# Strassen's scheme for layer B's V projection, woven with K's chunks, and K and V kept in DRAM

## The chip, the cores and the metric

The kernel runs on one core of one Trainium2 chip. The metric is the device time of one execution in microseconds (us). Engines are called as the profile calls them: PE is TensorE (PEld its weight loads), DVE VectorE, ACT ScalarE, POOL GpSimd, SP SyncE, which here only issues transfers.

## The reference, cut to what matters

A decoder trunk of two layers on 256 tokens of width 2048, all in 32-bit floats. Layer A is retention and attention to a memory of 256 tokens. Then one projection makes three keys and three values, which layer B's dilated attention reads:

```python
def shared_kv(x, g, w_kv):
    parts = split_cols(rmsnorm(x, g) @ w_kv, [DIL_W] * (2 * len(DIL_CONFIG)))

def dilated_layer(x, g, w_in, w_mem_kv, w_out, mem_n, kv):
    h = rmsnorm(x, g)
    parts = split_cols(h @ w_in, [DIL_W] * n_g + [DIL_W, MEM_W, MEM_W])
...
    for gi, (window, dil) in enumerate(DIL_CONFIG):
        q = parts[gi].reshape(B, S, DIL_HEADS, DIL_DH)
        o, lse = dilated_group(q, kv[2 * gi], kv[2 * gi + 1], dil, window // dil)
...
    return x + jnp.concatenate([o_dil, o_mem], axis=-1) @ w_out
```

K and V are each 256 x 2048 by 2048 x 6144. The norm is a row factor and a weight per column of x; both layer B's own norm and the one of K and V read the same x, with other weights.

## The kernel before, in words

**Numbers in two parts.** Every operand of a large product is split into a high part (ACT's cast to fp32r, line 94) and a low part (DVE's subtraction, line 95), and three products of parts are summed in PSUM: high by high, high by low, low by high.

**Chunks.** A projection is cut into chunks of 512 output columns. For one chunk eight weight tiles of 128 x 1024 come by SP's queue into a ring of six buffers (`raw`, RAW = 6), and each is split into `wh` and `wl`, rings of three (`wspl`). The splits are given AHEAD = 100 places of priority, so the scheduler puts them earlier in ACT's and DVE's streams than the work written before them.
- `dense_cols` (q, K, gates) gives features by tokens. It works in two halves of 256 features, with four weight tiles each; per tile eight pairs of a matmul of 512 columns (line 299) and one of 256 (line 301). A half ends with `fold`: ACT copies one part out of PSUM (344), DVE adds the other (345); K is then scaled by the tokens' norm (375). Two PSUM buffers, `acc0` and `acc1`, take turns.
- `dense` (V, gates of layer A, out-projections) gives tokens by features: per weight tile 12 matmuls of 512 columns (lines 316 to 318), then the scaled copies out of PSUM (385, 392, 393).

**Norm weights.** In layer B they are applied to the weights: `split_weights` runs in pieces of 256 or 512 columns with a factor per partition (lines 242, 243), once for GB and once for GK.

**Order.** For each of four head groups: q, K, q, K, q, K (seven chunks with the gate behind them), three V chunks, the gate. The attention of a group is a generator whose pieces `step()` sets between the next group's matmuls. `big` is a pool of 34 tiles of 512 KB in which x, the split x, K, V and what attention needs live.

Of the kernel before, what the change touches and what calls it, by code (L numbers as in the profile page):

```python
# [27 lines left out]
def yoco_trunk_kernel(  # L28
    ctx: ExitStack,
    tc: tile.TileContext,  # L30
    x, xt, memt,
    w_ac, w_ar, w_oa, w_b, w_ob, w_mk, w_mv, w_kc, w_vr,
    g_a, g_b, g_mem, g_kv, g_f,
# [11 lines left out]
    psum = ctx.enter_context(tc.tile_pool(name="psum", bufs=1, space=bass.MemoryType.PSUM))  # L45
    turns = {"acc": 0, "att": 0}

# [33 lines left out]
    def acc_tile(name=None):  # L81
        if name is None:
            name = ("acc0", "acc1")[turns["acc"] % 2]
            turns["acc"] += 1
        return psum.tile([P, 2, 2, S], F32, name=name)

    def bank():
        turns["att"] += 1
        if turns["att"] % 3 == 0:
            return acc_tile("acc2")[:, 0].rearrange("p h s -> p (h s)")  # L90
        return psum.tile([P, 512], F32, name="att", bufs=2)
# [20 lines left out]
    def drain():  # L112
        while pending:
            step()

    gain = const.tile([P, 4, KT], F32, name="gain")
# [173 lines left out]
    def dense_cols(xs, w, c, evict, g=None):  # L290
        for i in range(2):
            ps = acc_tile()
            for j in range(4):
                part = xs[j]
                for a, (wh, wl) in enumerate(weights(w[c, i, j], g, 4 * j, 4)):
                    first, last = j == 0 and a == 0, j == 3 and a == 3
                    for ct in range(2):
                        cs = slice(ct * P, (ct + 1) * P)
                        pe.matmul(ps[:, ct].rearrange("p h s -> p (h s)"), lhsT=wh[:, cs], rhs=xhl(part, a),  # L299
                                  start=first, stop=False, skip_group_check=True)  # L300
                        pe.matmul(ps[:, ct, 0, :], lhsT=wl[:, cs], rhs=xh(part, a),  # L301
                                  start=False, stop=last, skip_group_check=True)
# [60 lines left out]
    def cols_scaled(b, *job):  # L363
        o = big_tile()

        def evict(i, ps):
            fold(half(o, i), ps)
            if b is not None:
                scale_half(o, i, b)

# [244 lines left out]

    def turn_cols(xr, part):
        for i in range(2):
            ps = bank()
            for ct in range(2):
                for t in range(2):  # L620
                    cs = slice((2 * i + ct) * P, (2 * i + ct + 1) * P)
                    pe.transpose(ps[:, ct * S + t * P:ct * S + (t + 1) * P], xr[:, t, cs], ident)
            split(part[i][:, :, 0, :], part[i][:, :, 1, :], two(ps))
            yield

    n_m, n_x = Norm("m"), Norm("x")
# [66 lines left out]

    x1, ys = [], []
    part = const.tile([P, 2, 4], F32, name="part")
    ORDER = (4, 5, 0, 1, 2, 3)
    for c in range(4):
# [7 lines left out]
        x1.append(xr)  # L705
        ys.append(cols_pair())
        pending.append(turn_cols(xr, ys[c]))

    n_y = Norm("y")

    def norm_y():
# [6 lines left out]
        yield  # L718

    pending.append(norm_y())  # L720
    mkb2, mvb2 = {}, {}

    def split_big_rows(o):
        h, l = big_pair()
        h, l = rows(h), rows(l)
        f = "p t c -> p (t c)"
        split(h.rearrange(f), l.rearrange(f), o.rearrange(f))
        return h, l

    def split_kv(c):  # L730
        mkb2[c] = split_big(mk_b[c])
        yield
        h, l = split_big_rows(mv_b[c])
        mvb2[c] = (h, l)
        yield

    mix = SplitMix()
    for c in range(2):
        pending.append(split_kv(c))
        mq = cols_plain2(ys, w_b, 16 + c, GB)  # L740
        drain()
        gm = gate_cols(n_y.bh, ys, w_b, 18 + c, GB)
        pending.append(mem_attention(mq, mkb2[c], mvb2[c], gm, n_y, mix.tile(4 + c)))
    for hg in range(4):
        q, k, v = [], [], []
        for i in range(3):
            q.append((cols_plain2 if i == 0 else cols_plain)(ys, w_b, 4 * i + hg, GB))
# [7 lines left out]
        gt = gate_cols(n_y.bh, ys, w_b, 12 + hg, GB)  # L755
        pending.append(dilated(q, k, v, gt, n_y.nsd, mix.tile(hg)))

    part2 = const.tile([P, 2, 4], F32, name="part")

# [50 lines left out]
def _tables(np):  # L810
# [22 lines left out]

_ORDER = ["x", "xt", "memt", "w_ac", "w_ar", "w_oa", "w_b", "w_ob", "w_mk", "w_mv", "w_kc", "w_vr",
          "g_a", "g_b", "g_mem", "g_kv", "g_f", "rope", "decay", "mask"]
# [59 lines left out]
```

## Time and profile before

| | us |
|---|---|
| median of 3 runs (lowest, highest) | 1917.36 (1916.36, 1919.44) |
| the profiled execution's own time | 1918.47 |
| its span, first to last instruction | 1916.7 |
| busy in it: PE / PEld | 1900.3 / 1630.2 |
| DVE / ACT / POOL | 1240.2 / 1093.6 / 13.2 |
| mean granted clock of PE | 0.997 of full speed |

How to read it: busy time is the union of an engine's instructions. Matmuls overlap in the records (one of 512 columns has a mean of 390 ns, though they start closer together), so the pace of PE is read from how many start in a stretch. A mean over the whole span hides stages with other limits; so stretches are read by themselves.

### The profile page before, as it was taken

To read this page: it belongs to the slowest core of one execution; us is meant where nothing else is said; L and a number is where in the kernel's file an instruction comes from. 1 tells how busy PE (TensorE), PEld (TensorE's weight loads), DVE (VectorE), ACT (ScalarE), POOL (GpSimd) and SP (SyncE) were. 2 spreads that over 40 slices of the span, in tenths; PEclk is the share of its full clock that TensorE was granted. 3 is DMA by queue.
4 is the path that set the end of the run, shared out by engine and by line. 5 is a ranking of instruction groups with operands and counts; after the bars stand their busy time and mean duration, and the time that the engine had idled before them with its cause. 6 is when DMAs were issued, how large, how long until landed. Compare 5 with 4: busy or idle time off the path is not lost.

```text
span 1916.7 us, 27329 instructions
## 1 busy us (share of the span) xinstructions
PE 1900.3 (99%) x10136; PEld 1630.2 (85%) x10136; DVE 1240.2 (65%) x2191; ACT 1093.6 (57%) x2035; POOL 13.2 (1%) x24
## 2 busy tenths in 40 slices
PE   9999999999999999999999999999999999999998
PEld 7888888888888888888888988889888898888886
DVE  6566567557555457776656776567765777657654
ACT  6455444455444447766656666566665666656543
POOL 1000000000000000000000000000000000000000
PEclk9999999999999999999999999999999999999999
DMA  8565654655666665545665466654566546565463
GB/s 278 190 231 187 187 161 158 205 180 167 207 186 195 201 187 177 164 154 188 187 196 178 132 191 194 188 186 132 189 189 195 177 141 193 188 193 181 143 202 122
DMA packets 102805, 349.68 MB, mean 182 GB/s; under 512 B 11296, under 2 KB 17488, under 8 KB 102672
## 3 DMA queue, kind: packets, MB, share of 16 engines
q1 hardware_dynamic: 102208, 347.12, 57.4%
q8 instruction: 79, 1.29, 0.3%
q0 software_dynamic: 320, 0.81, 0.1%
q14 instruction: 54, 0.44, 0.1%
q10 hardware_dynamic: 144, 0.01, 0.0%
HBM read 345.80 MB, written 2.10 MB: 182 GB/s over the span
## 4 chain that ended last, share of the span: by engine, by line
PE 97%; DMA 1%; issue 1%; ACT 1%; DVE 1%; SPq 0%; POOL 0%; ACTq 0%; POOLq 0%; DVEq 0%
PE acc L299 33%; PE acc L301 17%; PE acc L318 13%; PE acc L317 13%; PE acc L316 13%; DMA raw<-in_w_mk_dram 1%; PE att L98 1%; PE att L100 1%; PE att L99 1%; PE att L599 1%; PE att L585 0%; PE att L563 0%; PE acc L100 0%; PE acc L99 0%; PE acc L98 0%
## 5 line engine op out<-in xcount | busy, mean ns | idle before, releaser
L299 PE MATMUL acc<-big,wh 128*128 128x512 f32 x2752 | 976.4, 399 | 2.0 <-DVE big L345 2.0
L301 PE MATMUL acc<-big,wl 128*128 128x256 f32 x2752 | 770.2, 280 | 0.0
L243 DVE SCALAR_TENSOR_TENSOR wl<-raw,gain,wh 128x256 fp32r<-128x256 f32 (+1 forms) x1216 | 567.4, 524 | 307.5 <-ACT wh L242 307.1
L242 ACT ACTIVATE wh<-raw,gain 128x256 fp32r<-128x256 f32 (+1 forms) x1216 | 567.2, 533 | 343.4 <-PE acc L299 176.9
L299 PEld LDWEIGHTS acc<-big,wh 128*128 128x128 f32 x2752 | 517.6, 188 | 122.5 <-DVE big L345 2.1
L95 DVE TENSOR_TENSOR wl<-raw,wh 128x1024 fp32r<-128x1024 f32 (+1 forms) x290 | 346.4, 1195 | 295.9 <-ACT wh L94 295.4
L301 PEld LDWEIGHTS acc<-big,wl 128*128 128x128 f32 x2752 | 519.7, 189 | 0.3
L94 ACT CAST wh<-raw 128x1024 fp32r<-128x1024 f32 (+1 forms) x290 | 298.1, 1028 | 380.0 <-PE acc L318 229.8
L316 PE MATMUL acc<-wh,big 128*128 128x512 f32 x1128 | 441.5, 391 | 0.0
L317 PE MATMUL acc<-wl,big 128*128 128x512 f32 x1128 | 439.6, 390 | 0.0
L318 PE MATMUL acc<-wh,big 128*128 128x512 f32 x1128 | 439.4, 390 | 0.0
L318 PEld LDWEIGHTS acc<-wh,big 128*128 128x128 f32 x1128 | 211.8, 188 | 44.0
L316 PEld LDWEIGHTS acc<-wh,big 128*128 128x128 f32 x1128 | 211.9, 188 | 43.2
L317 PEld LDWEIGHTS acc<-wl,big 128*128 128x128 f32 x1128 | 211.9, 188 | 42.6
L345 DVE TENSOR_TENSOR big<-acc,big 128x512 f32<-128x512 f32 x64 | 44.0, 689 | 0.0
L344 ACT COPY big<-acc 128x512 f32<-128x512 f32 x64 | 36.3, 568 | 0.7 <-PE acc L284 0.6
L95 DVE TENSOR_TENSOR big<-big 128x512 fp32r<-128x512 f32 (+1 forms) x34 | 28.0, 843 | 2.9 <-ACT big L94 2.8
L571 ACT ACTIVATE p<-sm,mn 128x512 f32<-128x512 f32 x32 | 23.1, 722 | 5.7 <-DVE mn L567 5.7
L94 ACT CAST big<-big 128x512 fp32r<-128x512 f32 (+1 forms) x34 | 24.3, 744 | 2.2 <-DVE big L601 2.0
L282 PE MATMUL acc<-big,wh 128*128 128x512 f32 x64 | 22.8, 400 | 1.3 <-ACT wh L94 1.3
L375 DVE TENSOR_TENSOR big<-big,nb 128x512 f32<-128x512 f32 x32 | 21.9, 691 | 1.0
L98 PE MATMUL att<-big 128*128 128x256 f32 x77 | 22.0, 286 | 0.0
(204 smaller groups left out, 930.9 us busy)
## 6 DMA issues: line engine op xcount, KB each, us to landing
raw<-in_w_b_dram SPq DMA_DIRECT2D x160, 512.0 KB, 3.5
raw<-in_w_kc_dram SPq DMA_DIRECT2D x96, 512.0 KB, 3.5
raw<-in_w_vr_dram SPq DMA_DIRECT2D x96, 512.0 KB, 3.5
raw<-in_w_ac_dram SPq DMA_DIRECT2D x64, 512.0 KB, 3.5
raw<-in_w_ar_dram SPq DMA_DIRECT2D x64, 512.0 KB, 3.5
raw<-in_w_oa_dram SPq DMA_DIRECT2D x48, 512.0 KB, 3.5
raw<-in_w_ob_dram SPq DMA_DIRECT2D x48, 512.0 KB, 4.1
raw<-in_w_mv_dram SPq DMA_DIRECT2D x32, 512.0 KB, 3.5
```

Source lines behind the costliest of these rows:

```text
L94: act.copy(hi, src)
L95: dve.tensor_tensor(lo, src, hi.bitcast(F32), ALU.subtract)
L98: pe.matmul(o, lhsT=ah, rhs=bh, start=first, stop=False, skip_group_check=True)
L242: act.activation(wh[:, cs], raw[:, cs], AF.Copy, scale=gs)
L243: dve.scalar_tensor_tensor(wl[:, cs], raw[:, cs], gs, wh[:, cs].bitcast(F32), ALU.mult, ALU.subtract)
L299: pe.matmul(ps[:, ct].rearrange("p h s -> p (h s)"), lhsT=wh[:, cs], rhs=xhl(part, a), start=first, stop=False, skip_group_check=True)
L301: pe.matmul(ps[:, ct, 0, :], lhsT=wl[:, cs], rhs=xh(part, a), start=False, stop=last, skip_group_check=True)
L316: pe.matmul(ps[t], lhsT=xh(part, a)[:, ts], rhs=wh, start=first, stop=False)
L317: pe.matmul(ps[t], lhsT=xh(part, a)[:, ts], rhs=wl, start=False, stop=False)
L318: pe.matmul(ps[t], lhsT=xl(part, a)[:, ts], rhs=wh, start=False, stop=last)
L344: act.copy(two(out), ps[:, :, 1, :])
L345: dve.tensor_tensor(two(out), ps[:, :, 0, :], two(out), ALU.add)
```

## The change

- V is computed by Strassen's scheme (in Winograd's form) on pairs of chunks: tokens in two halves of 128, the inner dimension in two of 1024, the columns in two of 512. Seven products of half size take the place of eight. The combinations of x (`combine`) are made once; those of the weights (`s1`, `w12 + w22`, `s2`, `s2 + w21`) by DVE for each pair, a quarter `d` at a time: three additions and four products for each of four `d` (first part), then one addition and three products for each of four (second part). PSUM banks `acc1` and `acc2` hold the sums; `p12` and `p` tiles the first combinations of results.
- All 12 K chunks come first, one after the other. From the second on, `weave` sets products between them: 2, 2, 1 and 0 behind a half's four weight tiles and 3 behind its fold. So a half has 8 products, and the 6 x 28 products fit into 21 of 22 halves. While products are left, K uses `acc0` alone, and `bank()` two buffers in place of three.
- K, V, x and the memory's K and V for layer B are stored to DRAM on POOL's queue (`spill`) and fetched by it (`fetch`) where they are used.
- Norm weights are applied to y (`Scaled`), for K and V and again for layer B; the weights are split whole, without a factor.

```diff
-            name = ("acc0", "acc1")[turns["acc"] % 2]
+            name = ("acc0", "acc1")[0 if woven else turns["acc"] % 2]
...
+                weave((2, 2, 1, 0)[j])
             evict(i, ps)
+            weave(3)
+
+    def strassen(parts, comb, w, r, done, banks=[]):
...
+        def product(ps, src, x, d, start, stop):
+            wh = wspl.tile([P, 1024], F32R, name="wh")
+            wl = wspl.tile([P, 1024], F32R, name="wl")
+            ahead(split, wh, wl, src)
+            for i in range(2):
+                h, l = x(2 * d + i)
+                cs = slice(i * 512, (i + 1) * 512)
+                first, last = start and i == 0, stop and i == 1
+                pe.matmul(ps, lhsT=h, rhs=wh[:, cs], start=first, stop=False, skip_group_check=True)
+                pe.matmul(ps, lhsT=h, rhs=wl[:, cs], start=False, stop=False, skip_group_check=True)
+                pe.matmul(ps, lhsT=l, rhs=wh[:, cs], start=False, stop=last, skip_group_check=True)
...
+        for d in range(4):
+            w11, w12, w22 = (load(q, d) for q in range(3))
+            s1, s2 = flat(big_tile()), flat(big_tile())
+            ahead(dve.tensor_tensor, s1, w11, w12, ALU.add)
+            ahead(dve.tensor_tensor, w12, w12, w22, ALU.add)
+            ahead(dve.tensor_tensor, s2, s1, w22, ALU.add)
+            keep.append(s2)
+            f, l = d == 0, d == 3
+            product(b0, w12, com(7), d, f, l)
...
+            product(b1, s1, com(5), d, f, l)
...
+            product(b2, w22, com(3), d, f, l)
+            yield
+            product(b3, w11, own(0, 0), d, f, l)
+            if l:
+                dve.tensor_tensor(c5, c5, b3, ALU.subtract)
+                dve.tensor_tensor(o1[:, 1, :], b3, c7, ALU.subtract)
+                dve.tensor_tensor(o2[:, 0, :], b2, c5, ALU.add)
+                dve.tensor_tensor(o2[:, 1, :], c7, c5, ALU.add)
+            yield
+        for d in range(4):
+            w21, s2 = load(3, d), keep[d]
+            product(b0, s2, com(6), d, f, l)
...
+            ahead(dve.tensor_tensor, s2, s2, w21, ALU.add)
+            product(b1, s2, own(1, 1), d, f, l)
...
+            product(b3, w21, own(1, 0), d, False, l)
...
+    def spill(t):
+        d = dram.tile([P, 1024], F32, name=f"spill{turns['spill']}")
+        pool.dma_start(out=d, in_=t)
...
+    for i in range(3):
+        for hg in range(4):
+            kd[i, hg] = spill(flat(cols_scaled(lambda: n_y.b, yk, w_kc, 4 * i + hg)))
+            if first:
+                drain()
+                first = False
+                for p in range(6):
+                    woven.append(strassen(yk, comb, w_vs[p], n_y.r, done(p)))
...
+    for j in range(4):
+        pending.append(yb.start(j))
...
-            kk = cols_scaled(n_y.b, ys, w_kc, 4 * i + hg, GK)
+            kk = fetch(kd[i, hg])
             k.append(split_big(kk) if i == 0 else kk)
-        for i in range(3):
-            v.append((rows_scaled2 if i == 0 else rows_scaled)(dense(ys, w_vr, 4 * i + hg, GK), n_y.r))
+            vv = fetch(vd[i, hg])
+            v.append(split_big_rows(vv) if i == 0 else rows(vv))
```

What it moves is seen in the built program's order. In the changed kernel's rows L97 is the subtraction of a split (95 before), L352 the additions of weight tiles, L457 fold's addition (345 before), L487 K's scaling (375 before), L310 and L312 a column chunk's matmuls (299 and 301 before), and L362 to L364 a product's.

First place, DVE where a K half ends. Before, four weight tiles are split between two folds (head group 0, K's first chunk and its second half):

```order
L243 SCALAR_TENSOR_TENSOR wl_8118<-raw_8115,gain_76,wh_8117 128x256 x4
L243 SCALAR_TENSOR_TENSOR wl_8151<-raw_8148,gain_76,wh_8150 128x256 x4
L243 SCALAR_TENSOR_TENSOR wl_8179<-raw_8176,gain_76,wh_8178 128x256 x4
L243 SCALAR_TENSOR_TENSOR wl_8207<-raw_8204,gain_76,wh_8206 128x256 x4
L345 TENSOR_TENSOR big_7913<-acc1_8030,big_7913 128x512
L375 TENSOR_TENSOR big_7913<-big_7913,nb_6094 128x512
```

Now, in the third K half among the first products: the first row is the split of that half's last weight tile (`raw_6468`), the fold stands near the end:

```order
L97 TENSOR_TENSOR wl_6471<-raw_6468,wh_6470 128x1024
L97 TENSOR_TENSOR wl_6494<-big_6453,wh_6493 128x1024
L97 TENSOR_TENSOR wl_6504<-raw_6451,wh_6503 128x1024
L352 TENSOR_TENSOR big_6552<-raw_6546,raw_6548 128x1024
L97 TENSOR_TENSOR wl_6514<-raw_6447,wh_6513 128x1024
L97 TENSOR_TENSOR wl_6527<-raw_6524,wh_6526 128x1024
L352 TENSOR_TENSOR big_6553<-big_6552,raw_6550 128x1024
L352 TENSOR_TENSOR raw_6548<-raw_6548,raw_6550 128x1024
L457 TENSOR_TENSOR big_6324<-acc0_6325,big_6324 128x512
L487 TENSOR_TENSOR big_6324<-big_6324,nb_6153 128x512
```

Between them now stand three products' splits (`wl_6494`, `wl_6504`, `wl_6514`), three additions, and the split of the next half's first tile (`wl_6527`).

Second place, PE at such an end. Before, the next half starts in the other PSUM buffer:

```order
L299 MATMUL acc0_7914<-big_6008,wh_8001 128x512
L301 MATMUL acc0_7914<-big_6008,wl_8002 128x256
L299 MATMUL acc0_7914<-big_6008,wh_8001 128x512
L301 MATMUL acc0_7914<-big_6008,wl_8002 128x256
L299 MATMUL acc1_8030<-big_5284,wh_8033 128x512
L301 MATMUL acc1_8030<-big_5284,wl_8034 128x256
```

Now three products stand between two K halves (the last of them here), and the next half writes `acc0` again, which the fold above has to leave first:

```order
L362 MATMUL acc2_6349<-wh_6513,big_5332 128x512
L363 MATMUL acc2_6349<-wl_6514,big_5332 128x512
L364 MATMUL acc2_6349<-wh_6513,big_5332 128x512
L362 MATMUL acc2_6349<-wh_6513,big_5332 128x512
L363 MATMUL acc2_6349<-wl_6514,big_5332 128x512
L364 MATMUL acc2_6349<-wh_6513,big_5332 128x512
L310 MATMUL acc0_6523<-big_5331,wh_6526 128x512
L312 MATMUL acc0_6523<-big_5331,wl_6527 128x256
```

So PE cannot begin a K half, as it did, while the former half is being read out.

Third place, DVE in the second part of a pair: the addition of `w21` stands one row ahead of the split of its sum, whose high part ACT casts in between:

```order
L97 TENSOR_TENSOR wl_7574<-big_7237,wh_7573 128x1024
L352 TENSOR_TENSOR big_7237<-big_7237,raw_7571 128x1024
L97 TENSOR_TENSOR wl_7585<-big_7237,wh_7584 128x1024
L97 TENSOR_TENSOR wl_7597<-raw_7594,wh_7596 128x1024
L97 TENSOR_TENSOR wl_7617<-raw_7571,wh_7616 128x1024
L97 TENSOR_TENSOR wl_7629<-raw_7626,wh_7628 128x1024
L97 TENSOR_TENSOR wl_7654<-big_7336,wh_7653 128x1024
L352 TENSOR_TENSOR big_7336<-big_7336,raw_7651 128x1024
L97 TENSOR_TENSOR wl_7670<-big_7336,wh_7669 128x1024
```

Before, no split waited for an addition; each followed a cast of a loaded tile.

## Rows read from the trace of the kernel before

**Rows 1.** Page: span, and each engine's busy time, share of the span, instructions.
```profile
span 1916.7 us, 27329 instructions
PE 1900.3 (99%) x10136; PEld 1630.2 (85%) x10136; DVE 1240.2 (65%) x2191; ACT 1093.6 (57%) x2035; POOL 13.2 (1%) x24
```

**Rows 2.** Windows, microseconds: out-projection A; a head group's K and q; its V; the next's K.
```profile
core 0: us, PE busy (x) PEld busy (x) DVE busy (x) ACT busy (x) POOL busy (x), PEclk, DMA share, GB/s
...
480.00:715.00 235.00, 233.79 (x1088) 194.60 (x1087) 128.53 (x142) 108.53 (x143) 2.73 (x4) 1.00 0.62 195
...
957.50:1022.70 65.20, 65.20 (x290) 54.01 (x289) 37.09 (x56) 35.66 (x57) 0.00 (x0) 1.00 0.61 193
1022.80:1195.40 172.60, 172.60 (x1041) 152.44 (x1041) 124.01 (x289) 116.01 (x272) 0.00 (x0) 1.00 0.55 171
1195.40:1260.70 65.30, 65.30 (x290) 54.09 (x289) 37.08 (x56) 35.64 (x57) 0.00 (x0) 1.00 0.60 193
```

**Rows 3.** Page part 4: the chain that ended last, by engine and by line.
```profile
PE 97%; DMA 1%; issue 1%; ACT 1%; DVE 1%; SPq 0%; POOL 0%; ACTq 0%; POOLq 0%; DVEq 0%
PE acc L299 33%; PE acc L301 17%; PE acc L318 13%; PE acc L317 13%; PE acc L316 13%; DMA raw<-in_w_mk_dram 1%; PE att L98 1%; PE att L100 1%; PE att L99 1%; PE att L599 1%; PE att L585 0%; PE att L563 0%; PE acc L100 0%; PE acc L99 0%; PE acc L98 0%
```

**Rows 4.** Windows of line 316 alone: one of three V matmuls, in two V stretches.
```profile
957.50:1022.70 65.20, 37.35 (x96) 17.96 (x96) 1.00 0.61 193
1195.40:1260.70 65.30, 37.36 (x96) 17.98 (x96) 1.00 0.60 193
```

**Rows 5.** Windows of line 299 alone: two column chunks of 64 wide matmuls each.
```profile
100.75:146.00 45.25, 45.20 (x128) 23.88 (x128) 1.00 0.69 233
```

**Rows 6.** DVE by line and shape: busy us, mean ns of one | idle before.
```profile
L243 DVE SCALAR_TENSOR_TENSOR wl<-raw,gain,wh 128x256 fp32r<-128x256 f32 x1024 | 431.7, 482 | 192.4 <-ACT wh L242 192.4
L95 DVE TENSOR_TENSOR wl<-raw,wh 128x1024 fp32r<-128x1024 f32 x274 | 335.4, 1224 | 293.1 <-ACT wh L94 292.7
...
L345 DVE TENSOR_TENSOR big<-acc,big 128x512 f32<-128x512 f32 x64 | 44.0, 689 | 0.0
...
L574 DVE TENSOR_SCALAR p<-p,rl 128x512 f32<-128x512 f32 x32 | 15.4, 483 | 0.6
...
L459 DVE TENSOR_SCALAR p<-p,rl 128x256 f32<-128x256 f32 x16 | 4.9, 348 | 0.1
...
L768 DVE TENSOR_TENSOR big<-big,p 128x512 f32<-128x512 f32 x8 | 5.2, 682 | 0.0
```

**Rows 7.** DVE in order of time: two operations of 1024 columns, back to back.
```profile
725.56 2.35 DVE L95 TENSOR_TENSOR big<-big 128x1024 fp32r<-128x1024 f32 x2
```

**Rows 8.** ACT by line and shape: casts of 1024 and 512 columns, PSUM copy.
```profile
L94 ACT CAST wh<-raw 128x1024 fp32r<-128x1024 f32 x274 | 288.3, 1052 | 376.9 <-PE acc L318 229.8 <-PE acc L299 103.1 <-issue 31.8
...
L344 ACT COPY big<-acc 128x512 f32<-128x512 f32 x64 | 36.3, 568 | 0.7 <-PE acc L284 0.6
...
L94 ACT CAST big<-big 128x512 fp32r<-128x512 f32 x24 | 13.9, 619 | 2.2 <-DVE big L601 2.0
```

**Rows 9.** Waits, whole span: us in total, times, longest us.
```profile
DVE wl L95 <- ACT wh L94: 295.4, 229, 3.5
ACT wh L94 <- PE acc L318: 229.8, 147, 2.2
```

**Rows 10.** DMA issues: count, KB each, median us to landing; POOL's own.
```profile
raw<-in_w_vr_dram SPq DMA_DIRECT2D x96, 512.0 KB, 3.5
...
mask_t<-in_mask_dram POOLq DMA_DIRECT2D x1, 512.0 KB, 7.0
...
L136 POOL DMA_DIRECT2D mask_t<-in_mask_dram x1 | 0.5, 536 | 0.0
```

**Rows 11.** Windows in the start: the granted clock is PEclk, behind POOL busy.
```profile
27.00:30.00 3.00, 3.00 (x19) 2.65 (x18) 2.90 (x6) 2.10 (x2) 0.00 (x0) 1.00 1.03 414
30.00:33.00 3.00, 1.03 (x8) 0.86 (x7) 2.26 (x5) 2.12 (x3) 1.64 (x1) 0.97 0.95 305
33.00:36.00 3.00, 2.97 (x9) 2.59 (x10) 2.10 (x4) 0.00 (x0) 0.00 (x0) 0.50 0.87 285
36.00:39.00 3.00, 3.00 (x17) 2.58 (x17) 0.44 (x1) 1.05 (x1) 0.00 (x0) 0.96 0.51 171
```

More of the change, by code (lines that the diff above doesn't have):

```diff
@@ L88, in bank @@
         turns["att"] += 1
-        if turns["att"] % 3 == 0:
+        if not woven and turns["att"] % 3 == 0:
             return acc_tile("acc2")[:, 0].rearrange("p h s -> p (h s)")
@@ L114, in drain, with weave @@
             step()
+    def weave(n=1):
+        for _ in range(n):
+            while woven:
+                try:
+                    next(woven[0])
+                    break
+                except StopIteration:
+                    woven.popleft()
     gain = const.tile([P, 4, KT], F32, name="gain")
@@ L304, in dense_cols, with combine @@
                         step()
+                weave((2, 2, 1, 0)[j])
             evict(i, ps)
+            weave(3)
+    def combine(raw, out):
+        for jj in range(2):
+            x11, x21 = raw[jj][:, :, 0:P], raw[jj][:, :, P:S]
+            x12, x22 = raw[jj + 2][:, :, 0:P], raw[jj + 2][:, :, P:S]
+            last = {}
+            for name, u, v in ((5, x21, x22), (7, x21, x11), (6, x11, 5), (3, x12, 6)):
+                d = tmp.tile([P, 4, P], F32, name=("sm", "p")[name % 2 if name != 5 else 0])
+                dve.tensor_tensor(d, u, last.get(v) if isinstance(v, int) else v, ALU.subtract)
+                last[name] = d
+                t = big.tile([P, 2, 4, P], F32R, name="big")
+                split(t[:, 0], t[:, 1], d)
+                out[name, jj] = t
+                yield
@@ L614, in dilated, with turn_cols @@
                 yield
-    def turn_cols(xr, part):
+    def turn_cols(xr, yt):
         for i in range(2):
@@ L718, in norm_y, with done, f @@
         yield
+    comb = {}
     pending.append(norm_y())
+    pending.append(combine(yk.raw, comb))
+    kd, vd = {}, {}
+    def done(p):
+        def f(o1, o2):
+            for n, o in ((2 * p, o1), (2 * p + 1, o2)):
+                vd[n // 4, n % 4] = spill(o.rearrange("p t c -> p (t c)"))
+        return f
+    first = True
+    for i in range(3):
[6 more added lines that the diff above has]
+                    woven.append(strassen(yk, comb, w_vs[p], n_y.r, done(p)))
+    while woven:
+        weave()
     mkb2, mvb2 = {}, {}
@@ L724, in split_big_rows @@
         h, l = big_pair()
[L725 to L728, printed above, removed]
+        split(flat(h), flat(l), flat(o))
+        return rows(h), rows(l)
     def split_kv(c):
-        mkb2[c] = split_big(mk_b[c])
+        mkb2[c] = split_big(fetch(mk_b[c]))
         yield
-        h, l = split_big_rows(mv_b[c])
-        mvb2[c] = (h, l)
+        mvb2[c] = split_big_rows(fetch(mv_b[c]))
         yield
+    for j in range(4):
+        pending.append(yb.start(j))
     mix = SplitMix()
@@ L754, in yoco_trunk_kernel @@
             pending.append(mix.halves(5))
-        gt = gate_cols(n_y.bh, ys, w_b, 12 + hg, GB)
+        gt = gate_cols(n_y.bh, yb, w_b, 12 + hg)
         pending.append(dilated(q, k, v, gt, n_y.nsd, mix.tile(hg)))
+    x1 = [rows(fetch(d)) for d in x1]
     part2 = const.tile([P, 2, 4], F32, name="part")
```

108 lines of the change are left out of this document (92 added, 16 removed).

## The prediction

> **What bounds the kernel now.** I read the page's busy times first: PE is busy for 1900.3 of 1916.7 us, DVE for two thirds of that [rows 1]. Then the chain of work that ended last: 97% of it is PE, four fifths in the matmuls of chunks [rows 3]. Then stretches by themselves, because a mean hides the stage that changes: in layer B PE is busy for the whole of a V stretch (65.2 of 65.2 us) and of the K and q stretch behind it (172.6 of 172.6), at full granted clock, while DVE is busy for 57% and 72% [rows 2]. So every matmul taken away is worth its pace, as long as ACT and DVE still deliver split weights in time. That is the question: Strassen's scheme pays for fewer matmuls with additions on DVE.
>
> **Paces.** A V stretch holds three chunks, 96 matmuls of each of three lines, 288 in 65.2 us: 0.2264 us each [rows 4]. Two column chunks take 45.25 us [rows 5], so one takes 22.6, a half 11.3, a weight tile of it 2.82 us. A product is six matmuls of 512 columns: 6 x 0.2264 = 1.36 us. On DVE one subtraction of 1024 columns lasts 1.22 us [rows 6], but two in a row take 2.35 [rows 7]: operations overlap by 0.09, so one costs 1.13 us. One of 512 columns lasts 0.69 [rows 6], by the same overlap 0.60. The additions of weight tiles (1024 columns, SBUF to SBUF, plain floats) have no row of their own; the nearest are the subtractions of the same size, and at 512 columns the plain float product of two SBUF tiles takes 0.68, the subtraction's time [rows 6]. A gain is excluded only as far as DVE's single-input operation is no guide: it takes 0.48 at 512 columns [rows 6]. I take 1.13; the low end is 0.48/0.69 of it, 0.79, which would give back 96 x 0.34 = 33 us of DVE.
>
> **What is removed.** V's 12 chunks had 12 x 96 = 1152 matmuls, six pairs now have 6 x 28 x 6 = 1008: 144 x 0.2264 = **-32.6 us** of PE.
>
> **What DVE now has.** A K half: 4 x 1.13 + 2 x 0.60 = 5.7 us (its pieces with a factor were 4 x 0.48 per tile [rows 6], so K is cheaper than it was). A pair: 16 additions and 28 subtractions of 1024 columns, 8 operations of 512 on results: 44 x 1.13 + 8 x 0.60 = 54.5 us. The woven stage is 21 halves and six pairs: DVE 21 x 5.7 + 6 x 54.5 = 447 us, PE 21 x 11.3 + 168 x 1.36 = 466 us. DVE would have to work for 96% of the time that PE needs, in bursts: a tile of K costs PE 2.82 and DVE 1.13, a product of the first part PE 1.36 and DVE 1.13 + 3/4 x 1.13 = 1.98. With rings of three high and three low tiles, DVE can be two tiles ahead and no more.
>
> **What that exposes.** I set PE and DVE against each other between two points of each half, by the rows of the order. First stretch: from the split of a half's last tile to the end of its fold. PE has that tile and three products there, 2.82 + 4.08 = 6.9 us, and then must wait, since the next half writes `acc0` again. DVE has, in the example shown, seven operations of 1024 columns and the fold: 7 x 1.13 + 0.60 = 8.5 us, 1.6 too many. Over the 20 whole halves in the woven part of the order it has between 4.0 and 10.8 us; 13 are over 6.9, by 22.4 us together. Second stretch: from the fold to the split of the next half's last tile. PE has three tiles and five products, 15.3 us, DVE between 8.0 and 18.8; 8 of 20 are over, by 16.6 us. Together **+39.0 us**. A short stretch doesn't pay for a long one, because DVE can't run two tiles ahead through a fold that waits for PE.
>
> On top come ACT's casts. A cast of 1024 columns takes 1.05 us [rows 8]; it waits for PE to free a high tile, and the subtraction waits for the cast, as the waits already show where nothing hangs on it [rows 9]. In a stretch where DVE is late, a cast in the chain is no longer hidden; in the second part of a pair the split even stands right behind the addition that its cast waits for. Nothing (ACT always ahead) and two per stretch (42 casts, 44 us) bound it; I take one for each of the 21 late stretches, **+22.1 us**, since ACT has only 84 + 168 casts of 1.05 us, 265 us, beside DVE's 447.
>
> **Start and end.** The first product waits for three additions and a split, 4 x 1.13 = 4.5 us, beside one K tile of 2.8: **+1.7**. After the last K half the first piece of the other scaled y is made behind the fold: two scalings of 256 columns (0.35 each), a cast (0.62), a subtraction (0.69) [rows 6, 8]: **+2.3**.
>
> **What costs nothing.** Splitting layer B's q and gate weights whole takes 1.22 in place of 4 x 0.48 us per tile off DVE, but PE is the bound there (172.6 of 172.6), so nothing is won [rows 2]. Scaling y for K and V and `combine` add to DVE 16 x 0.35 + 24 x 0.69 = 22 us; most of it lies in the out-projection of layer A, where DVE is idle for 106 of 235 us [rows 2]; without that cover it would cost its 22. As many weight tiles as before come by SP's queue. The 64 stores and fetches go by POOL's queue, where an issue takes 0.54 us [rows 10] and POOL is busy for 13 us in all [rows 1]; the DMA engines are busy for 0.55 to 0.62 of layer B [rows 2]. A fetch of that queue landed in 7.0 us [rows 10] and is needed one group later; only the eight that are split at once stand in DVE's stream. I take 0 for them, at most 8 x 7.0. The attention of a group has 20 pieces, for which the next group's four chunks have 64 places; it stays between matmuls.
>
> **Sum:** -32.6 + 39.0 + 22.1 + 1.7 + 2.3 = +32.5. On the profiled execution's 1918.5 us this is 1951.0; the median shown lies 1.1 below it, so I say **1950 us**. K and V together, 12 x 22.6 + 4 x 65.2 = 532 us before, would take 564.
>
> **Rivals.**
> - *The bursts even out, faster.* If DVE is two tiles ahead whenever a burst begins, neither stretch is late, and PE stays the bound: -32.6 + 1.7 + 2.3 = -28.6, 1889 us; half evened out gives some 1905. What decides is DVE's idle time in the woven stage: over 466 - 447 = 19 us, and PE waits. For it: the sums, in which DVE is still below PE, and additions at the low end. Against: the order, where the fold stands behind additions for later products, and one buffer for K.
> - *It cancels.* Exposed times of about 29 us give 1917: the two stretches without most casts.
> - *Loads come late, slower still.* A quarter `d` holds three of the six raw buffers until its fourth product is split. In the order the next `w12` is loaded into the former one's buffer, with two or three DVE operations (2.3 to 3.4 us) before its use, and a load takes 3.5 us [rows 10]: 0.1 to 1.2 us for each of 24 quarters, at most 29 more: 1979. For it: SP's queue is in order, so one late load delays those behind it; against: the additions stand far ahead.
> - *The clock falls.* In the start PE was busy for 1.03 of 3 us, and in the next 3 us the granted clock was 0.50, the lower of its two levels (1.2 GHz), then 0.96 [rows 11]: 0.5 x 3 + 0.04 x 3 = 1.6 us lost per such pause. My longest fold waits are 10.8 - 6.9 = 3.9 us, in three or four halves. If each of 20 folds does it: +32, 1982. Against: most waits are shorter than that pause.
>
> The Trainium skill, "TensorE: Matmul & The Clock Gate", section "HAM oscillation — how this bites in real kernels", says that waits between groups of matmuls put the array back to half rate, each time anew; by that rule this rival's 1982 would be the time. The trace agrees in that one place at the start, with 0.50; no row shows it for waits of one or two us.
>
> **Numbers.** My forecast has a chance of 0.62, with 1930 to 1970 as its own range (casts from none to two). Evened out and faster 0.14, cancelled 0.06, late loads 0.12, clock 0.06. A measurement of this kernel can tell about 0.2%, 4 us, from no change. So slower 0.62 + 0.12 + 0.06 = 0.80, same 0.06, faster 0.14. A range of 1905 to 1980 leaves out the fully evened case (0.09) and the upper half of the two slow rivals (0.09).
>
> **What would show it.** Right: 1008 matmuls in the products; in the woven stage PE busy for some 88% and DVE for some 85 to 90%; waits of the column matmuls for the fold on DVE, 1 to 4 us long, and of products for splits; K and V in about 564 us, every other stage as before. Wrong: PE over 97% busy there (evened out); weight additions waiting for DMA by more than a few us in sum (late loads); a granted clock below 0.97 there (clock); a longer stretch in layer B's q chunks or the end (fetches).

## The result, and the profile after

The changed kernel takes **1969.45 us** (median of 4 runs, 1968.2 to 1973.05), the one before 1917.66 in the same comparison: a ratio of 1.0272, 95% interval 1.0255 to 1.029. It is slower, by 51.8 us; 1950 was forecast, +32.5 us.

First the page of the changed kernel: span, busy time of each engine, and the chain that ended last, by engine and line. They answer to [rows 1, 3].

```profile
span 1966.1 us, 25978 instructions
...
PE 1900.6 (97%) x9992; PEld 1609.2 (82%) x9992; DVE 1340.3 (68%) x1595; ACT 995.1 (51%) x1283; POOL 47.9 (2%) x88
...
PE 85%; DVE 7%; issue 3%; DMA 3%; ACT 2%; SPq 0%; POOL 0%; ACTq 0%; DVEq 0%; POOLq 0%
```

PE runs 144 instructions fewer, as it should, and is as long busy as before in a span that is 49.4 us longer. The chain that was 97% PE has now 15% of other links. Where they lie is seen in windows of the same kernel (columns as in [rows 2]): the out-projection of layer A, the first K chunk with the first additions, the woven stage, its end, and layer B's q chunks and attention.

```profile
482.50:715.00 232.50, 231.29 (x1073) 192.53 (x1072) 129.13 (x146) 109.28 (x142) 4.36 (x7) 1.00 0.63 201
715.20:743.50 28.30, 26.63 (x157) 23.10 (x157) 27.80 (x47) 18.16 (x28) 1.61 (x2) 1.00 0.52 168
743.50:1287.80 544.30, 498.32 (x2365) 401.00 (x2366) 463.13 (x442) 290.78 (x310) 11.74 (x22) 0.98 0.60 196
1287.80:1310.00 22.20, 19.32 (x110) 16.49 (x109) 19.05 (x30) 14.19 (x20) 3.73 (x7) 1.00 0.93 328
1310.00:1808.50 498.50, 498.28 (x3034) 441.57 (x3033) 303.60 (x404) 246.88 (x348) 14.46 (x27) 1.00 0.60 195
```

Out-projection and layer B are PE's as before; layer A ends at 715.2 us, and it ended at 715.1. Nearly all of the loss lies in the woven stage. Its work on PE can be worked out: 678 pairs of column matmuls, 2.82 / 8 us each by [rows 5], and 1008 product matmuls at 0.2264 us [rows 4] make 239 + 228 = 467 us. The stage lasts 544.3, so 77 us are lost in it. With 1.7 us of PE's idle time ahead of it and 2.9 behind it 81.6 us are lost and 32.6 us of matmuls saved, 49.0 of the span's 49.4. DVE is busy for 85% of the stage, and the granted clock is 0.98 in the mean.

What PE waited for there, by line and shape (busy us, mean ns of one | idle before and what ended it):

```profile
L310 PE MATMUL acc<-big,wh 128*128 128x512 f32 x679 | 253.4, 410 | 19.1 <-DVE big L457 16.8 <-ACT wh L96 2.1 <-ACT p L386 0.2
L312 PE MATMUL acc<-big,wl 128*128 128x256 f32 x678 | 195.3, 288 | 5.7 <-DVE wl L97 5.5
L363 PE MATMUL acc<-wl,big 128*128 128x512 f32 x336 | 135.1, 402 | 6.7 <-DVE wl L97 6.6
L362 PE MATMUL acc<-wh,big 128*128 128x512 f32 x336 | 134.8, 402 | 16.2 <-ACT wh L96 7.8 <-DVE big L403 4.2 <-DVE big L457 1.7
L364 PE MATMUL acc<-wh,big 128*128 128x512 f32 x336 | 132.4, 395 | 0.0
```

The two halves of the forecast are both here: column matmuls wait for the fold's addition (L457, 16.8 us), and all kinds wait for splits or casts of weights. From the same stage, waits by engine (us in total, times, longest us; the first answers to [rows 9]):

```profile
DVE wl L97 <- ACT wh L96: 68.0, 89, 2.8
ACT wh L96 <- DVE big L352: 39.9, 19, 3.5
ACT wh L96 <- DVE raw L352: 29.0, 13, 4.1
PE acc L310 <- DVE big L457: 16.8, 9, 2.6
DVE raw L352 <- DMA raw<-in_w_vs_dram: 5.2, 7, 1.2
DVE big L352 <- DMA raw<-in_w_vs_dram: 5.2, 7, 1.0
```

DVE waits for casts, and casts wait for DVE's weight additions (68.9 us in two rows), so where one of the two is late the other is too. For loads DVE waits only 10.4 us in all.

One such place in order of time (start, us, then the instruction, idle before it in brackets):

```profile
911.82 0.40 PE L364 MATMUL acc<-wh,big 128*128 128x512 f32 x1
912.90 1.22 DVE L352 TENSOR_TENSOR big<-raw 128x1024 f32<-128x1024 f32 x1
914.04 0.68 DVE L457 TENSOR_TENSOR big<-acc,big 128x512 f32<-128x512 f32 x1
...
914.87 0.77 PE L310 MATMUL acc<-big,wh 128*128 128x512 f32 x1 [2.65 <-DVE big L457]
...
915.64 0.63 PE L310 MATMUL acc<-big,wh 128*128 128x512 f32 x1
```

A weight addition for a later product stands ahead of the fold's (L457), and PE starts no matmul for 3.05 us. Behind the pause its wide matmuls start 0.64 us apart (915.64, 916.28) and not 0.35: the clock has fallen. Windows around it (PEclk is the third number from the right, as in [rows 11]):

```profile
910.60:913.60 3.00, 1.45 (x5) 0.86 (x5) 3.00 (x4) 1.23 (x2) 0.00 (x0) 1.00 0.19 51
913.60:920.40 6.80, 5.46 (x16) 4.31 (x16) 5.12 (x6) 1.24 (x2) 0.00 (x0) 0.50 0.45 143
920.40:923.90 3.50, 0.00 (x0) 0.00 (x0) 2.62 (x4) 1.61 (x3) 0.00 (x0) 0.99 0.32 129
923.90:927.30 3.40, 2.95 (x7) 2.37 (x8) 2.22 (x3) 1.29 (x2) 0.53 (x1) 0.50 0.38 152
```

Half rate, 1.2 GHz, holds for 6.8 us, and after the next pause for 3.4 more. In the woven stage there are six such falls (at 913.6, 923.9, 1026.3, 1101.4, 1132.1 and 1234.5), 23.9 us together.

### The profile page after: what moved, and what is told of

Same layout as the page of the kernel before. It is cut to its first block, busy times and chain, and to the rows that moved or that the text cites. A ratio compares the mean times of both kernels' runs of the same rounds, so it can differ in the third digit from the quotient of the medians.

```text
span 1966.1 us, 25978 instructions
## 1 busy us (share of the span) xinstructions
PE 1900.6 (97%) x9992; PEld 1609.2 (82%) x9992; DVE 1340.3 (68%) x1595; ACT 995.1 (51%) x1283; POOL 47.9 (2%) x88
## 4 chain that ended last, share of the span: by engine, by line
PE 85%; DVE 7%; issue 3%; DMA 3%; ACT 2%; SPq 0%; POOL 0%; ACTq 0%; DVEq 0%; POOLq 0%
PE acc L310 30%; PE acc L312 15%; PE acc L429 9%; PE acc L430 9%; PE acc L428 9%; DVE wl L97 4%; PE acc L363 2%; DMA raw<-in_w_vs_dram 2%; PE acc L364 2%; PE acc L362 2%; DVE big L352 2%; ACT wh L96 2%; PE att L102 1%; PE att L100 1%; PE att L101 1%
## 5 line engine op out<-in xcount | busy, mean ns | idle before, releaser
L97 DVE TENSOR_TENSOR wl<-raw,wh 128x1024 fp32r<-128x1024 f32 (+1 forms) x642 | 773.7, 1210 | 511.9 <-ACT wh L96 510.9
L96 ACT CAST wh<-raw 128x1024 fp32r<-128x1024 f32 (+1 forms) x642 | 666.2, 1040 | 752.4 <-PE acc L310 352.1
L310 PE MATMUL acc<-big,wh 128*128 128x512 f32 x2752 | 991.9, 402 | 23.9 <-DVE big L457 21.7
L312 PE MATMUL acc<-big,wl 128*128 128x256 f32 x2752 | 777.3, 283 | 5.7 <-DVE wl L97 5.5
L310 PEld LDWEIGHTS acc<-big,wh 128*128 128x128 f32 x2752 | 522.2, 190 | 152.5 <-issue 18.7
L312 PEld LDWEIGHTS acc<-big,wl 128*128 128x128 f32 x2752 | 525.3, 191 | 13.7 <-DVE wl L97 10.7
L428 PE MATMUL acc<-wh,big 128*128 128x512 f32 x744 | 292.4, 393 | 0.0
L429 PE MATMUL acc<-wl,big 128*128 128x512 f32 x744 | 290.6, 391 | 0.0
L430 PE MATMUL acc<-wh,big 128*128 128x512 f32 x744 | 290.4, 390 | 0.0
L430 PEld LDWEIGHTS acc<-wh,big 128*128 128x128 f32 x744 | 139.8, 188 | 28.9
L428 PEld LDWEIGHTS acc<-wh,big 128*128 128x128 f32 x744 | 139.9, 188 | 28.1
L429 PEld LDWEIGHTS acc<-wl,big 128*128 128x128 f32 x744 | 139.9, 188 | 27.5
L362 PE MATMUL acc<-wh,big 128*128 128x512 f32 x336 | 134.8, 402 | 16.2 <-ACT wh L96 7.8
L363 PE MATMUL acc<-wl,big 128*128 128x512 f32 x336 | 135.1, 402 | 6.7 <-DVE wl L97 6.6
L364 PE MATMUL acc<-wh,big 128*128 128x512 f32 x336 | 132.4, 395 | 0.0
L96 ACT CAST wh<-big 128x1024 fp32r<-128x1024 f32 x72 | 75.7, 1051 | 85.3 <-DVE big L352 39.9
L97 DVE TENSOR_TENSOR wl<-big,wh 128x1024 fp32r<-128x1024 f32 x72 | 88.0, 1223 | 26.2 <-ACT wh L96 25.8
L362 PEld LDWEIGHTS acc<-wh,big 128*128 128x128 f32 x336 | 63.5, 189 | 36.7 <-ACT wh L96 14.9
L363 PEld LDWEIGHTS acc<-wl,big 128*128 128x128 f32 x336 | 63.6, 189 | 24.6 <-DVE wl L97 12.9
L364 PEld LDWEIGHTS acc<-wh,big 128*128 128x128 f32 x336 | 63.6, 189 | 12.9
L352 DVE TENSOR_TENSOR big<-big,raw 128x1024 f32<-128x1024 f32 x48 | 58.5, 1220 | 0.4
L97 DVE TENSOR_TENSOR big<-big 128x512 fp32r<-128x512 f32 (+1 forms) x54 | 43.8, 824 | 2.3 <-ACT big L96 1.7
```

The lines of the kernel that those rows point to most:

```text
L96: act.copy(hi, src)
L97: dve.tensor_tensor(lo, src, hi.bitcast(F32), ALU.subtract)
L352: f(*args)
L362: pe.matmul(ps, lhsT=h, rhs=wh[:, cs], start=first, stop=False, skip_group_check=True)
L363: pe.matmul(ps, lhsT=h, rhs=wl[:, cs], start=False, stop=False, skip_group_check=True)
L364: pe.matmul(ps, lhsT=l, rhs=wh[:, cs], start=False, stop=last, skip_group_check=True)
```

## The experiments

The theory: the sum of DVE's work isn't the bound, but its bursts are; a fold stands behind additions while K has one PSUM buffer, and rings of three let DVE run two tiles ahead at most. The rivals: the reordering, the stores and fetches, or the norm on y cost the time; the additions are simply too much for DVE; the loads come late; the clock takes it. The interval behind each ratio to the kernel before is in brackets. "Woven stage" is the time from 743.5 us to the last product.

**1. V without Strassen's scheme, the rest of the change kept** (only `combine`, which the products alone need, goes with it).

```diff
-    pending.append(combine(yk.raw, comb))
...
-                for p in range(6):
-                    woven.append(strassen(yk, comb, w_vs[p], n_y.r, done(p)))
-    while woven:
-        weave()
+    for n in range(12):
+        o = rows_scaled(dense(yk, w_vs, n), n_y.r)
+        vd[n // 4, n % 4] = spill(o.rearrange("p t c -> p (t c)"))
```

> K first, stores and fetches, and the scaled y stay; V's 12 chunks are made by the plain scheme of the kernel before, after K, and nothing is woven. Bursts theory (DVE's additions and splits, in bursts, make PE wait): with 12 plain V chunks PE is the bound again, the matmuls are those of before, so the time is that of before plus the start and end of the stage: 1917 to 1925 us. Rival (the new order, the 64 transfers on POOL's queue and the second scaling of y cost something themselves): 1935 us or more.

Measured: 1921.80 us, ratio 1.0019 [1.0009, 1.0029]. K and V and the end, 715 to 1266 us, are PE's almost alone, and PE has one wait there (waits of PE from 715 to 1290 us):

```profile
715.00:1266.00 551.00, 546.92 (x2794) 465.76 (x2793) 288.93 (x290) 244.10 (x266) 16.83 (x31) 1.00 0.69 217
```
```profile
PE acc L310 <- DVE big L97: 4.1, 1, 4.1
```

That wait is the first q chunk's for the other scaled y. It covers the whole difference of 3.6 us. So K's order, the 64 transfers by POOL's queue and the factors on y cost nothing else; what is lost comes with the products and what is made for them.

**2. The weight additions left out, every product and split kept.** A product takes a loaded tile in place of a sum, so V is not the reference's.

```diff
-            s1, s2 = flat(big_tile()), flat(big_tile())
-            ahead(dve.tensor_tensor, s1, w11, w12, ALU.add)
-            ahead(dve.tensor_tensor, w12, w12, w22, ALU.add)
-            ahead(dve.tensor_tensor, s2, s1, w22, ALU.add)
-            keep.append(s2)
+            s1 = w12
...
-            w21, s2 = load(3, d), keep[d]
+            w21 = load(3, d)
+            s2 = w21
...
-            ahead(dve.tensor_tensor, s2, s2, w21, ALU.add)
```

> Leaves out the 96 additions of weight tiles (each product takes a loaded tile in place of the sum), so V is not the reference's; matmuls, splits, loads and weaving stay. Bursts theory: DVE has 96 x 1.13 = 108 us less in the woven stage, 338 us for PE's 466, no burst is longer than what PE has to do beside it, the fold comes in time: 1890 to 1910 us, and the granted clock stays at 1.00. Rival (one PSUM buffer for K is the cost, whatever DVE does): the fold is still needed before each half, at least half of the loss against before stays: 1940 us or more.

Measured: 1906.32 us, 0.994 [0.9925, 0.9955]. The woven stage of this run, and its wide column matmuls:

```profile
743.50:1226.10 482.60, 474.77 (x2363) 395.17 (x2364) 357.29 (x347) 293.74 (x309) 11.78 (x22) 1.00 0.67 220
```
```profile
L310 PE MATMUL acc<-big,wh 128*128 128x512 f32 x679 | 243.7, 398 | 2.1 <-ACT wh L96 1.4 <-DVE big L453 0.5 <-ACT p L382 0.2
```

DVE loses 106 us of work there, the stage 61.7 us, and the clock no longer falls in it. The wait for the fold (L453 here) goes from 16.8 to 0.5 us. So nearly all of the loss hangs on the additions. Whether it is their sum or their place, this run can't tell; the next ones can.

**3. A second PSUM buffer for K.** Every second half of a woven K chunk uses attention's two banks, idle at that time; DVE's additions stay.

```diff
-            ps = acc_tile()
+            if woven and i:
+                ps = [psum.tile([P, 2, S], F32, name="att", bufs=2) for _ in range(2)]
+                pv = ps
+            else:
+                ps = acc_tile()
+                pv = [ps[:, 0], ps[:, 1]]
...
```

> Every second K half in the woven stage is summed in the two small PSUM buffers, which nothing uses there, in place of the one buffer; its fold is then in four pieces of 256 columns. Bursts theory: the six waits of 3 us at the start of a half go (16.8 us) and the clock falls that follow some of them (six of 1.7 us), but DVE's work is still in bursts, which then make products and tiles wait: 1938 to 1955 us. Rival (the one PSUM buffer is the cost): PE would be the bound, 1890 to 1905 us.

Measured: 1945.95 us, 1.0147 [1.0132, 1.0162], 23.5 us less than the changed kernel, 20.5 of them in the woven stage. Lines of its woven stage, as a window and by line:

```profile
743.50:1267.30 523.80, 493.71 (x2375) 399.22 (x2376) 463.69 (x452) 291.64 (x321) 11.78 (x22) 0.99 0.63 204
```
```profile
L367 PE MATMUL acc<-wh,big 128*128 128x512 f32 x335 | 134.9, 404 | 16.3 <-ACT wh L96 8.7 <-DVE big L408 6.3 <-DVE big L398 1.3
L315 PE MATMUL acc<-big,wh 128*128 128x512 f32 x344 | 125.4, 402 | 1.5 <-ACT wh L96 1.5
```

No column matmul waits for a fold any more (L315 was L310), with DVE as busy as before: for this wait it was the place, not the sum. What stays is the products' own wait for casts and for results leaving their bank (L367 was L362, 16.2 us then). The time at half rate went from 23.9 to 13.7 us, so a few of the 23.5 us are the clock's.

**4. Idle matmuls to keep the clock up, first try.** Seven matmuls ahead of the six halves behind the long pauses.

```diff
+                if turns["half"] in (2, 6, 8, 12, 16, 20):
+                    fp = psum.tile([P, 512], F32, name="att", bufs=2)
+                    for _ in range(7):
+                        pe.matmul(fp, lhsT=xh(xs[0], 0)[:, 0:P], rhs=xhl(xs[0], 0), start=True, stop=True, skip_group_check=True)
```

> Seven idle matmuls of 512 columns (7 x 0.2264 = 1.6 us) are put ahead of the six K halves that waited 3 us, into a PSUM buffer that nothing reads; all waits stay. If the falls of the granted clock behind those waits cost what the rows say (four or five falls of 1.7 us, 7 to 9 us): 1958 to 1964 us, granted clock 0.99 or more in the woven stage. If the falls are only a mark of waits that would be paid anyway: 1967 to 1973 us.

Measured: 1967.57 us, 1.0261 [1.0246, 1.0277]. It tells nothing: these matmuls depend on nothing new, and the scheduler set them all between 740 and 826 us. Five of the six pauses stayed.

**5. The same, tied to the last product's low tile.**

```diff
...
-                    for _ in range(7):
-                        pe.matmul(fp, lhsT=xh(xs[0], 0)[:, 0:P], rhs=xhl(xs[0], 0), start=True, stop=True, skip_group_check=True)
+                    fh, fl = turns["last"]
+                    for _ in range(9):
+                        pe.matmul(fp, lhsT=fh, rhs=fl[:, 512:1024], start=True, stop=True, skip_group_check=True)
```

> Nine idle matmuls (9 x 0.2264 = 2.0 us) that read the last product's low weights, so that they can only run behind it, stand ahead of the six K halves that waited 3 us; they write a PSUM buffer that nothing reads. The waits for the fold end when they ended. If a fall of the granted clock behind such a wait costs what the rows say (3.4 us at half speed, some 1.7 us, and what late matmuls pass on): 1955 to 1963 us, with the falls behind these halves gone. If the falls only mark waits that are paid anyway: 1967 to 1973 us.

Measured: 1965.31 us, 1.0248 [1.0231, 1.0265]. At those six halves the clock no longer falls; in one of them, where 1026.3 began a stretch at 0.50:

```profile
1023.00:1030.00 7.00, 6.42 (x33) 5.13 (x32) 5.58 (x7) 4.20 (x5) 0.00 (x0) 1.00 0.46 146
```

But it does in three other places of the stage, 13.7 us in all, one of them new (1160.3), and once behind it (1293.4). The woven stage is 540.5 us, 3.8 less, for 10.2 us less at half rate: 0.37 us lost per microsecond (PE isn't busy through all of it). By that the 23.9 us cost some 9, an estimate from one trace of each kernel, and at most 12 (half of them). The time lies outside both ranges, between them: the gain is smaller than was expected, and the clock can't be the main cause.

**6. Rings of four for the split weights** (`big` gives up two of its tiles).

```diff
-BIG = 34
+BIG = 32
...
-    wspl = ctx.enter_context(tc.tile_pool(name="wspl", bufs=3))
+    wspl = ctx.enter_context(tc.tile_pool(name="wspl", bufs=4))
```

> Rings of four split weight tiles in place of three (the pool of 34 large tiles is cut to 32 for it); one PSUM buffer for K and the additions stay. Bursts theory (DVE has time enough in sum, 447 us for PE's 466, and fails because it can be two tiles ahead at most, with the cast in the chain): one tile more hides the casts, 1930 to 1950 us. Rival (DVE's sum is the bound, and rings don't matter): 1960 us or more.

Measured: 1936.22 us, 1.0098 [1.0083, 1.0113]: 33.2 us less than the changed kernel. One tile more of lead is worth more than the second PSUM buffer. PE's wait for the fold shrinks as well, from 16.8 to 3.8 us; presumably DVE comes to the fold less late (wide column matmuls of the woven stage):

```profile
L310 PE MATMUL acc<-big,wh 128*128 128x512 f32 x685 | 250.2, 403 | 8.6 <-ACT wh L96 4.5 <-DVE big L457 3.8
```

**7. Both (the second PSUM buffer and rings of four), and the products spread evenly**: two behind each tile, none behind the fold; the last is the edit shown.

```diff
-                weave((2, 2, 1, 0)[j])
+                weave((2, 2, 2, 2)[j])
             evict(i, ps)
-            weave(3)
+            weave(0)
```

> Two PSUM buffers for K, rings of four, and two products behind each of a half's four weight tiles in place of 2, 2, 1, 0 and 3 behind the fold. Bursts theory: with bursts of two products and a fold that nobody waits for, PE comes close to its own 466 us in the woven stage: 1895 to 1915 us, faster than the kernel before. Rival (the additions on DVE cost their time wherever they stand): 1925 us or more.

Measured: 1912.35 us, 0.997 [0.9959, 0.9981]. With all of DVE's additions in place the loss is gone: 57.1 us less than the changed kernel, where the two parts alone gave 23.5 and 33.2.

**8. The additions on POOL**, which stands nearly idle.

```diff
-            ahead(dve.tensor_tensor, s1, w11, w12, ALU.add)
-            ahead(dve.tensor_tensor, w12, w12, w22, ALU.add)
-            ahead(dve.tensor_tensor, s2, s1, w22, ALU.add)
+            ahead(pool.tensor_tensor, s1, w11, w12, ALU.add)
+            ahead(pool.tensor_tensor, w12, w12, w22, ALU.add)
+            ahead(pool.tensor_tensor, s2, s1, w22, ALU.add)
...
-            ahead(dve.tensor_tensor, s2, s2, w21, ALU.add)
+            ahead(pool.tensor_tensor, s2, s2, w21, ALU.add)
```

> The 96 additions of weight tiles run on POOL in place of DVE; all else as in the change. If POOL adds 1024 columns in 3 us or less (96 x 3 = 288 us, beside 544 us of the woven stage) and leaves DVE alone, DVE has 338 us for PE's 466: 1900 to 1925 us. If POOL's and DVE's accesses hold each other up, DVE's subtractions take clearly longer than 1.22 us, and the time is 1950 us or more; no row here shows either yet.

Measured: 2031.83 us, 1.0599 [1.0578, 1.0619], 62 us worse. Groups of POOL by line in the whole span, one group of DVE in the woven stage (the changed kernel's, then this run's), and that stage as a window:

```profile
L352 POOL TENSOR_TENSOR big<-big,raw 128x1024 f32<-128x1024 f32 x48 | 133.4, 2781 | 175.6 <-DVE wl L97 140.1 <-issue 35.4
L352 POOL TENSOR_TENSOR raw<-raw 128x1024 f32<-128x1024 f32 x24 | 73.1, 3045 | 16.8 <-DMA raw<-in_w_vs_dram 15.3
```
```profile
L97 DVE TENSOR_TENSOR wl<-raw,wh 128x1024 fp32r<-128x1024 f32 x182 | 219.2, 1220 | 42.6 <-ACT wh L96 42.2
L97 DVE TENSOR_TENSOR wl<-raw,wh 128x1024 fp32r<-128x1024 f32 x181 | 322.5, 1800 | 82.3 <-ACT wh L96 75.6 <-DMA raw<-in_w_kc_dram 6.0
```
```profile
743.50:1352.50 609.00, 514.91 (x2368) 403.28 (x2367) 478.49 (x347) 290.24 (x310) 272.66 (x114) 0.96 0.52 174
```

POOL's spans are rough, but POOL takes over twice DVE's 1.22 us for an addition, and DVE's own subtractions become longer: 1800 ns in the mean of the woven stage, against 1220 in the same stage of the changed kernel. DVE is busy for 478 us of the stage with 95 instructions fewer. So DVE is held up while POOL adds; whether POOL is too can't be told, since no run has its additions alone. How much of the 62 us comes from that, from POOL's longer additions (casts wait 109.4 us for them) and from 44.4 us at half rate, this run doesn't split. The Trainium skill, "SBUF — State Buffer", section "Who interferes with whom", says that a VectorE instruction with two SBUF inputs contends with a GpSimd instruction that reads SBUF; the trace agrees, with 1800 ns against 1220.

**9. Rings of six, with everything of the seventh run**, `big` at 28 tiles.

```diff
-BIG = 32
+BIG = 28
...
-    wspl = ctx.enter_context(tc.tile_pool(name="wspl", bufs=4))
+    wspl = ctx.enter_context(tc.tile_pool(name="wspl", bufs=6))
```

> As the run with two PSUM buffers for K and two products behind each tile, but with rings of six split tiles in place of four (the pool of large tiles cut to 28). Bursts theory: three additions in a row (3.4 us of DVE) no longer empty the ring, what remains is start, end and single waits: 1893 to 1905 us. Rival (what is left, 12 us over the sum of PE's own work, is DVE's additions as such): 1908 us or more.

Measured: 1896.58 us, 0.9893 [0.9876, 0.9909], beside 1917.50 for the kernel before: faster than both kernels. Its page, the woven stage as a window, and two of PE's lines in that stage:

```profile
PE 1875.7 (99%) x9992; PEld 1604.8 (85%) x9992; DVE 1331.0 (70%) x1606; ACT 984.2 (52%) x1294; POOL 48.0 (3%) x88
...
PE 95%; issue 2%; DVE 2%; ACT 1%; DMA 0%; POOL 0%; SPq 0%; ACTq 0%; POOLq 0%
```
```profile
743.50:1219.30 475.80, 472.40 (x2363) 396.01 (x2362) 454.89 (x450) 281.27 (x320) 11.74 (x22) 1.00 0.68 227
```
```profile
L315 PE MATMUL acc<-big,wh 128*128 128x512 f32 x344 | 123.2, 397 | 1.1 <-ACT wh L96 1.1
L367 PE MATMUL acc<-wh,big 128*128 128x512 f32 x336 | 131.5, 397 | 0.0
```

DVE works for 455 of 476 us, 96%, and PE hardly waits; the stage is within 9 us of the 467 that PE's work needs. DVE's sum was never the bound.

**10. Rings of four and the even spread, but one PSUM buffer.**

```diff
-                weave((2, 2, 1, 0)[j])
+                weave((2, 2, 2, 2)[j])
             evict(i, ps)
-            weave(3)
+            weave(0)
```

> Rings of four and two products behind each tile, but one PSUM buffer for K, and no product behind the fold. The next half then has only the two products behind the last tile, 2.7 us, to cover its fold. Bursts theory: the fold is waited for at most of the 21 halves, some 0.5 to 1.5 us each, so 15 to 25 us over the same kernel with two buffers: 1925 to 1940 us. Rival (one buffer costs nothing once bursts are even): 1910 to 1918 us.

Measured: 1931.51 us, 1.0069 [1.0054, 1.0084] (`wspl` and BIG as in the sixth run). Against the sixth run the spread gives 4.7 us, against the seventh the one buffer costs 19.2. Two of PE's lines in the woven stage:

```profile
L310 PE MATMUL acc<-big,wh 128*128 128x512 f32 x664 | 240.0, 400 | 3.6 <-ACT wh L96 3.4
L362 PE MATMUL acc<-wh,big 128*128 128x512 f32 x336 | 135.6, 407 | 9.1 <-DVE big L410 2.9 <-ACT wh L96 2.2 <-DVE big L393 2.0
```

The time came as expected, the reason for it did not, so the hit is luck: in the stage no column matmul waits for a fold, and their weight loads wait for one 1.7 us in all. Only the first q chunk behind the stage waits, in a pause of 3.2 us. What is left is products that wait for their own results to leave their bank (L410, L393), for casts and for splits, and 13.7 us at half rate where the seventh run has 3.4. How a second buffer for K takes these away isn't shown.

## Why the prediction was right, and what it missed

**Sign and mechanism: right.** The additions turn DVE's work into bursts, and what decides is the lead, not the sum. The second run shows that the loss hangs on the additions, the third, sixth, seventh and ninth that it shrinks and in the end is gone with all of them in place, and the first that nothing else of the change costs more than one wait of 4.1 us. Of the signs named ahead, PE's 92% of the stage (88 were named), DVE's 85% and waits for the fold of at most 2.6 us came; K and V took 581.9 us to the first q matmul and not 564. The granted clock, 0.98 in the mean, stayed above the sign for that rival, and yet it cost time.

**PE's gain, -32.6: right.** The 1008 matmuls run at the pace of [rows 4]: in the ninth run the woven stage is 475.8 us, where those paces make 467.

**DVE's prices: right.** An addition takes 1220 ns in the trace, as the subtraction does; the low end of 0.79 is out. DVE was to be busy for 447 us there and was for 463.

**The two stretches and the casts, 39.0 + 22.1 = 61.1: about right.** From the starts of the 2365 matmuls of the woven stage, 50 gaps over 0.5 us (over 1.0 at half rate) hold 54.9 us beyond the pace, and smaller delays make up the rest of the 77 us that the clock doesn't explain, some 13. The first part, folds behind additions, was 22.4 us; rows of the trace put 16.8 down to it, and taking the fold out of the way was worth 23.5 us, with the half-rate time and the pause at the end that went with it. Fewer folds were late than the 13 halves of the sum: the row counts 9 waits. The second part and the casts can't be told apart by these runs: a ring of four takes 33.2 us away, but it helps both, and part of the fold's wait too. The cast as such is confirmed only as a link (DVE waits 68.0 us for it in the stage, and casts in turn 68.9 for additions).

**Start and end, +1.7 and +2.3: right in size.** PE is idle for 1.7 of the 28.3 us in which the first additions are made, but not from them alone: without them, in the second run, the pause in front of the first product is 0.8 us in place of 1.7. `combine` stands there too, and not in the out-projection of layer A, where the forecast had most of that work covered: DVE is busy for 27.80 of the 28.30 us. At the end the changed kernel has a pause of 3.2 us, the first experiment one of 4.1. The four parts named for the end add up to 2.0, not 2.3.

**What costs nothing: right, but for the place of `combine`.** In layer B's q chunks and attention PE is busy for 498.28 of 498.50 us, and POOL is busy for 48 us in all and has 0% of the chain.

**The clock: the term that the sum left out.** In the sum it stood at nothing, and as a rival at 0.06, with the words "most waits are shorter than that pause". The waits were listed, up to 3.9 us, and there were pauses of 3 us or more at six K halves and once among the products (4.4 us). In the woven stage the clock fell six times: behind four of these halves, at the pause among the products, and near one of 2.35 us. By the fifth run's estimate the falls cost some 9 us, 12 at most. That is over half of the 16.9 us by which the span's growth (49.4) exceeds the forecast (32.5); the other 5 to 8 are presumably small delays, which the two-stretch sum didn't count. The rival's price of 1.6 us per fall agrees (9 / 6 = 1.5), its twenty falls don't. The forecast had the pieces: three or four longest waits of up to 3.9 us, at 1.6 us each, are 5 to 6 us that belonged in the sum. The Trainium skill, "TensorE: Matmul & The Clock Gate", section "HAM oscillation — how this bites in real kernels", was cited for falls at each wait between groups, which would have given 1982; the trace agrees in six places of the stage, but not each time anew: two of the six pauses of 3 us (764.9 and 863.6) kept full rate.

**The rivals.** Late loads: 10.4 us of DVE's waits are for loads, against 29 us of PE's time in the rival, and a load of the new weights takes 4.2 us against 3.5. The bursts evening out by themselves: no; they had to be evened out by hand, and the time then was 1912 to 1897, in the last case between that rival's 1905 and 1889. (Half of the exposed 61.1 us over 1889 would be 1919; 1905 has only the second stretch, 16.6. And the five lines of the chain make 89%, not four fifths; nothing hangs on it.)

## What to carry to other kernels

An algorithm that trades matmuls for vector work has to be judged over the distance that the vector engine may run ahead, not over the stage: here DVE, with work for 455 to 463 us beside PE's 467, loses 52 us with a lead of two tiles and a single PSUM buffer, and wins 21 with a lead of five, two buffers and the products spread evenly. Ask first where the read-out of a PSUM buffer stands in the vector engine's stream and what stands ahead of it. In this kernel four of six pauses of TensorE of 3 us had a fall of the clock behind them: count such pauses as themselves, and ask what the clock may add.

## What was not expected of the hardware

Pauses that look the same to PE don't end the same. At two K halves (start of the pause to its end, then what follows):

```profile
764.90:767.90 3.00, 0.35 (x3) 0.04 (x1) 2.96 (x4) 0.64 (x1) 0.00 (x0) 1.00 0.84 270
767.90:774.90 7.00, 7.00 (x36) 5.93 (x37) 5.74 (x6) 4.52 (x5) 0.00 (x0) 1.00 0.44 115
...
1023.20:1026.20 3.00, 0.43 (x2) 0.00 (x1) 2.96 (x5) 0.59 (x1) 0.00 (x0) 1.00 0.98 320
1026.30:1029.70 3.40, 3.40 (x11) 2.93 (x12) 2.80 (x3) 1.30 (x2) 0.00 (x0) 0.50 0.35 86
```

PE was busy for 0.35 us of the one pause and 0.43 of the other, and only behind the second did the clock fall; the pause at 863.6 us (3.03 us from start to start) kept it as well. At 1101.4 it fell 2.7 us behind a pause of only 2.35 us (1096.4 to 1098.7), with two gaps of 1 us in between. In the fourth run the pause at 911.6, of 3.05 us, kept the clock that the changed kernel lost at that place (911.8). These runs don't show what decides. The other surprise is the eighth run's: an engine that stood idle made the busy one slower, and the kernel 62 us slower than with the additions on the busy one.
